# Odd mixer of a two-layer network: the norm's factor in the stream, the gate read from its bank, softplus as a scale

## Chip, cores and metric

The kernel runs on one core of a Trainium2 chip. What counts is the device time of one execution in microseconds (us). Matmuls run on TensorE (PE in the rows), the other work on VectorE (DVE), ScalarE (ACT) and GpSimd (POOL); SyncE (SP) issues most DMAs.

## The reference

The network takes 512 tokens of 1024 channels in fp32 through an even mixer, an odd mixer and other blocks around them. The change is in the odd mixer. Cut to what matters:

```python
def odd_mixer(h, w_in, conv_w, conv_b, w_rg, b_rg, w_ig, b_ig, lam, w_out):
    p = einsum("btd,dn->btn", h, w_in)            # h is rmsnorm(h, g): h * rsqrt(mean(h*h) + eps) * g
    xr, gate = split(p, [1536], axis=-1)
    xc = causal_depthwise_conv(xr, conv_w, conv_b)          # 4 taps
    r = sigmoid(per_head(xc, w_rg) + b_rg)                  # 12 heads of 128
    i = sigmoid(per_head(xc, w_ig) + b_ig)
    log_a = -8.0 * r * softplus(-lam)
    a = exp(log_a)
    mult = sqrt(-expm1(2.0 * log_a))
    bterm = mult * (i * xc)
    hs = scan(a, bterm)                                     # h_t = a_t * h_(t-1) + b_t
    y = hs * silu(gate)
    return einsum("btn,nd->btd", y, w_out)
```

## The kernel before

**Layout.** Activations stand transposed: a tile is 128 channels by 512 tokens, so the stream of 1024 channels is 8 tiles, and each of the 12 heads is one tile. Every fp32 matmul is made of three: an operand is split in a rounded high part and the rest, and `mm3` (lines 303 to 310) multiplies high by high (308), high by low (309) and low by high (310). A head's input projection is `mtile`: 8 tiles by 3, so 24 matmuls into one bank.

**Weights.** A chunk of weights is loaded by SyncE's queue into one of two raw buffers (line 288), cast on ScalarE to its high part (`hi<-raw`, recorded at the helper's line 249), and its low part is a subtraction, in this stage on GpSimd (`lo<-raw,hi`, helper line 252). hi and lo have three buffers each; the small gate weights of a head (`wrh`, `wrl`) one. The kernel asks for a chunk three ahead of its use.

**The odd stage** is `odd`, from line 733. The stream times g is split in 8 tiles xg, each with a high and a low part. The squares of h are summed, PE turns the sum into columns (line 368), VectorE makes the reciprocal root `rs_s` of them, PE spreads it (line 397), and ScalarE copies it to the tile `rs`, the norm's factor for each token. The loop runs over 12 heads with a lag of 3: head n+3's projection goes into one of three "mm" banks, is multiplied by `rs` in the bank, convolved (one ScalarE activation and three VectorE steps that read the bank, `xc<-mm,vecs,xc`) and split to `xs`; then for head n the two gate products r and i (6 matmuls, two "sp" banks), two sigmoids, the product of r by `sp4` (4 times softplus) and of i by xc on GpSimd, and the gate projection into one of two "yp" banks (24 matmuls), which VectorE multiplies by `rs` into `gt`.

After each second head `lru` (line 787) does the recurrence of two heads on tiles of 1024, the 12 heads making six groups, 0 to 5. On ScalarE: tanh of the gate, tanh and exp of x, sqrt. On VectorE: two steps `u<-u,e`, two products for x, two scans (line 808), the product with the gate, and the split to y. x, i and gt have two buffers; e and u have one. ScalarE needs another table for sigmoid, exp and sqrt (ACT_TABLE_LOAD), while tanh goes with more than one of them.

The out-projection follows: 8 output tiles of two weight chunks each, first the chunks of heads 0 to 5 for seven of the tiles (the first half), then those of heads 6 to 11 (the second half). It reuses the banks of all three names.

**Order of the work.** Instructions are put on the engines' queues by a scheduler with a timeline of its own (line 1822), not in the order of the code; `lru` is put behind by `later`. Each engine then works strictly in its order. A small change in the code can so move many instructions, and the section on the change shows what stands where.

## Time and profile before

| | |
|---|---|
| runs shown | 1882.61, 1886.52, 1893.18 us; median 1886.52 |
| profiled execution | 1886.16 us; its span 1884.3 us |
| granted TensorE clock, mean of the span | 0.963 |
| TensorE busy | 1764.2 us (94%) |
| VectorE busy | 1167.2 us (62%) |
| ScalarE busy | 762.0 us (40%) |
| GpSimd busy | 456.6 us (24%) |
| the odd stage | 425.7 to 697.9 us of the span |

The profile is of one execution. Start times are counted from the first instruction; the span leaves out the 1.86 us around it. A row of a timeline gives the start, the duration, the engine, the kernel's line, the operation, the tiles (written <- read), and in brackets how long the engine was idle before it and what it waited for. A row with x3 stands for three instructions that follow each other. Rows of waits and groups give sums. Successive instructions of an engine overlap a little, so the distance between two starts is shorter than the duration.

### The profile page before, as it was taken

The page shows a single profiled execution, that of the slowest core. Times are in us where ns is not written, and L with a number is a line of the kernel's source. Part 1 is how long each engine was busy: PE and PEld are TensorE (multiplying, and loading weights), DVE is VectorE, ACT ScalarE, POOL GpSimd, SP SyncE. Part 2 cuts the span into 40 slices and gives each one's busy share as a digit, 9 for nine tenths or more (in the row PEclk, how much of TensorE's full clock was granted, in tenths as well). Part 3 has the DMA queues.
Part 4 walks back from the last instruction along what each step waited for, and adds up shares of the span by engine and source line. Part 5 has one row for each costly group of instructions (what it writes and reads, how often), then busy time and mean ns, then how long its engine had stood idle before and what let it go on. Part 6 is the DMA issues. An engine that isn't in the chain of part 4 may idle for free.

```text
span 1884.3 us, 24650 instructions
## 1 busy us (share of the span) xinstructions
PE 1764.2 (94%) x9298; PEld 1439.7 (76%) x9298; DVE 1167.2 (62%) x1885; ACT 762.0 (40%) x1330; POOL 456.6 (24%) x422
## 2 busy tenths in 40 slices
PE   7797999999887897899999999998999999999997
PEld 5685778877765776687888888887778888888886
DVE  9989777555888859655432344578686642244456
ACT  4334444443554462234432332335665432233234
POOL 5464667333666643100000000032000000000002
PEclk8898999999988898899999999999999999999998
DMA  4598443331222488523232222333111233322322
GB/s 167 136 225 213 128 129 123 119 104 65 76 75 76 136 244 291 169 92 112 93 100 91 100 100 91 101 106 110 41 55 45 101 101 91 100 101 91 100 94 91
DMA packets 128871, 215.93 MB, mean 115 GB/s; under 512 B 40048, under 2 KB 79728, under 8 KB 128752
## 3 DMA queue, kind: packets, MB, share of 16 engines
q1 hardware_dynamic: 108144, 189.27, 32.5%
q10 hardware_dynamic: 17968, 16.43, 2.6%
q0 software_dynamic: 2640, 8.65, 1.4%
q8 instruction: 73, 1.20, 0.3%
q14 instruction: 46, 0.38, 0.1%
HBM read 187.44 MB, written 26.21 MB: 113 GB/s over the span
## 4 chain that ended last, share of the span: by engine, by line
PE 68%; DVE 14%; issue 5%; POOL 4%; ACT 4%; DMA 3%; SPq 1%; ACTq 0%; DVEq 0%; POOLq 0%
PE mm L308 19%; PE mm L310 19%; PE mm L309 19%; POOL lo L252 2%; DVE lo L252 1%; DVE e L808 1%; ACT hi L249 1%; PE pv L1609 1%; SPq L1175 1%; PE sc L309 1%; PE sc L308 1%; PE sc L310 1%; DVE pl L264 1%; DVE srm L267 1%; DVE h L264 1%
## 5 line engine op out<-in xcount | busy, mean ns | idle before, releaser
L249 ACT ACTIVATE hi<-raw 128x1024 fp32r<-128x1024 f32 (+1 forms) x280 | 292.4, 1046 | 672.8 <-PE mm L309 552.4
L252 DVE TENSOR_TENSOR lo<-raw,hi 128x1024 fp32r<-128x1024 f32 (+1 forms) x211 | 262.1, 1243 | 422.1 <-ACT hi L249 417.3
L310 PE MATMUL mm<-xg,lo 128*128 128x512 f32 x924 | 361.0, 391 | 9.4 <-DVE lo L252 8.1
L308 PE MATMUL mm<-xg,hi 128*128 128x512 f32 x924 | 363.2, 394 | 5.1 <-ACT hi L249 1.8
L309 PE MATMUL mm<-xg,hi 128*128 128x512 f32 x924 | 360.2, 390 | 0.3 <-DVE xg L252 0.2
L1423 POOL DMA_DIRECT2D pj<-proj x16 | 8.8, 549 | 1025.8 <-DVE t L264 784.0
L308 PE MATMUL mm<-hid,hi 128*128 128x512 f32 (+1 forms) x648 | 250.7, 387 | 1.8 <-DVE t L252 1.8
L309 PE MATMUL mm<-hid,hi 128*128 128x512 f32 (+1 forms) x648 | 250.3, 387 | 0.0
L310 PE MATMUL mm<-hid,lo 128*128 128x512 f32 (+1 forms) x648 | 250.1, 386 | 0.0
L310 PEld LDWEIGHTS mm<-xg,lo 128*128 128x128 f32 x924 | 173.8, 188 | 48.0 <-DVE lo L252 9.0
L308 PEld LDWEIGHTS mm<-xg,hi 128*128 128x128 f32 x924 | 173.8, 188 | 44.9 <-ACT hi L249 2.3
L252 POOL TENSOR_TENSOR lo<-raw,hi 128x1024 fp32r<-128x1024 f32 (+1 forms) x69 | 170.6, 2473 | 146.8 <-ACT hi L249 140.6
L309 PEld LDWEIGHTS mm<-xg,hi 128*128 128x128 f32 x924 | 173.8, 188 | 36.4 <-DVE xg L252 1.4
L308 PEld LDWEIGHTS mm<-hid,hi 128*128 128x128 f32 x648 | 121.7, 188 | 26.6 <-DVE t L252 2.0
L310 PEld LDWEIGHTS mm<-hid,lo 128*128 128x128 f32 x648 | 121.7, 188 | 24.6
L309 PEld LDWEIGHTS mm<-hid,hi 128*128 128x128 f32 x648 | 121.7, 188 | 24.6
L308 PE MATMUL mm<-y,hi 128*128 128x512 f32 x192 | 78.6, 409 | 10.2 <-ACT y L249 8.9
L309 PE MATMUL mm<-y,hi 128*128 128x512 f32 x192 | 76.8, 400 | 0.0
L310 PE MATMUL mm<-y,lo 128*128 128x512 f32 x192 | 76.5, 399 | 0.0
L309 PE MATMUL mm<-big,hi 128*128 128x512 f32 x160 | 64.5, 403 | 3.9 <-DVE big L264 3.9
L308 PE MATMUL mm<-big,hi 128*128 128x512 f32 x160 | 65.3, 411 | 2.2 <-ACT hi L249 2.2
L310 PE MATMUL mm<-big,lo 128*128 128x512 f32 x160 | 64.2, 402 | 0.1
(468 smaller groups left out, 3086.1 us busy)
## 6 DMA issues: line engine op xcount, KB each, us to landing
raw<-in_w_up SPq DMA_DIRECT2D x64, 512.0 KB
raw<-in_w_down SPq DMA_DIRECT2D x64, 512.0 KB
raw<-in_w_in_even SPq DMA_DIRECT2D x40, 512.0 KB
raw<-in_w_in_odd SPq DMA_DIRECT2D x24, 512.0 KB
raw<-in_w_out_even SPq DMA_DIRECT2D x16, 512.0 KB
raw<-in_w_glu SPq DMA_DIRECT2D x16, 512.0 KB
raw<-in_w_gate SPq DMA_DIRECT2D x16, 512.0 KB
raw<-in_w_out_odd SPq DMA_DIRECT2D x16, 384.0 KB
```

Source lines behind the costliest of these rows:

```text
L249: self.nc.scalar.activation(out=out, in_=in_, func=func, scale=scale, bias=bias)
L252: (eng or self.nc.vector).tensor_tensor(out=out, in0=a, in1=b, op=op)
L264: self.nc.vector.scalar_tensor_tensor(out=out, in0=a, scalar=s, in1=b, op0=op0, op1=op1)
L267: (eng or self.nc.vector).tensor_scalar(out=out, in0=a, scalar1=s1, scalar2=s2, op0=op0, **({} if op1 is None else {"op1": op1}))
L308: mm(out, hi[:, sl], xh, start=start, stop=False)
L309: mm(out, hi[:, sl], xl, start=False, stop=False)
L310: mm(out, lo[:, sl], xh, start=False, stop=stop)
L808: nc.vector.tensor_tensor_scan(out=y, data0=u[:, k], data1=x[:, k], initial=0.0, op0=ALU.mult, op1=ALU.add)
L1175: nc.sync.dma_start(out=M0[:, 128 * g:128 * g + 128], in_=bass.AP(k0.tensor, k0.offset + 4096 * g, [[16, 8], [256, 16], [1, 128]]))
L1423: self.nc.gpsimd.dma_start(out=p, in_=pj[m])
L1609: mm(o, l, r[:, w], start=n == 0, stop=n == 6 * nk - 1)
```

## The change

Three things in `odd` and `lru`:

- The first four heads (0 to 3) still read the raw stream, which now lies in the buffers of y, and are multiplied by `rs` in the bank. After head 0's convolution the code makes a second stream, `xn`, split from h times g times `rs` (8 products, 8 casts, 8 subtractions); heads 4 to 11 and all gate projections read it and are not multiplied any more. The new lines at the top of `odd` only allocate tiles, which fixes their addresses.
- The gate's tanh reads the bank directly, per head, and one VectorE step makes (tanh + 1) times the bank. The product by `rs` and the tanh and product of 1024 in `lru` are gone.
- GpSimd's product of x by `sp4` is gone. tanh and exp in `lru` run per head, on 512 tokens, with a column of `sp4` as the activation's scale; `sp4` has 24 columns, 12 for tanh and 12 for exp.

```diff
     def odd(self, h):
         nc = self.nc
-        xg = [self.split(h[k], self.X(), self.V("g_odd", k)) for k in range(8)]
+        for t, b, w in (("acc", 2, T), ("xr", self.XR, T), ("rs", 1, T), ("xc", 2 + self.LAG, T), ("xs", 2 + 2 * self.LAG, T), ("wrh", 1, 256),
+                        ("wrl", 1, 256), *((t, b, self.G * T) for t, b in (("x", 2), ("i", 2), ("gt", 2), ("e", 1), ("u", 1)))):
+            self.L(t, b, F32, (128, w))
+        xg = [self.split(h[k], self.LR("y", 24), self.V("g_odd", k)) for k in range(8)]
...
-                self.mul(px, px, rs)
+                if n <= self.LAG:
+                    self.mul(px, px, rs)
...
+                if n == 0:
+                    xn = []
+                    for k in range(8):
+                        if k % 2 == 0:
+                            t2 = self.L("gt", 2, F32, (128, G, T))
+                        t = t2[:, k % 2]
+                        self.stt(t, h[k], self.V("g_odd", k), rs, ALU.mult, ALU.mult)
+                        xn.append(self.split(t, self.X()))
+                if n == self.LAG:
+                    xg = xn
                 n -= self.LAG
...
-            self.ts(x, x, self.sp4[:, n:n + 1], ALU.mult, 0.0, ALU.add, eng=nc.gpsimd)
             self.mul(i, i, xc, nc.gpsimd)
             pg = self.mtile(xg, "yp")
-            self.mul(gt, pg, rs)
+            self.act(gt, pg, AF.Tanh, scale=0.5)
+            self.stt(gt, gt, 1.0, pg, ALU.add, ALU.mult)
             if n % G == G - 1:
                 with self.later(self.LRU):
-                    ysp += self.lru(*grp)
+                    ysp += self.lru(n - G + 1, *grp)
...
-    def lru(self, x, i, gt):
+    def lru(self, n, x, i, gt):
...
-        self.act(u, gt, AF.Tanh, scale=0.5)
-        self.stt(gt, u, 1.0, gt, ALU.add, ALU.mult)
-        self.act(u, x, AF.Tanh)
-        self.act(e, x, AF.Exp, scale=-2.0)
+        for k in range(self.G):
+            self.act(u[:, k], x[:, k], AF.Tanh, scale=self.sp4[:, n + k:n + k + 1])
+        for k in range(self.G):
+            self.act(e[:, k], x[:, k], AF.Exp, scale=self.sp4[:, 12 + n + k:13 + n + k])
         self.act(x, u, AF.Sqrt)
...
-        self.sp4 = C("sp4", 12)
-        self.ts(self.sp4, q, 4.0, ALU.mult)
+        self.sp4 = C("sp4", 24)
+        self.ts(self.sp4[:, 0:12], q, 4.0, ALU.mult)
+        self.ts(self.sp4[:, 12:24], q, -8.0, ALU.mult)
```

How the scheduler places this is seen at three places. In the names of the rows, `sp_628` is `sp4` and `vecs` holds constants.

**The start of the stage.** VectorE before, from the end of the reciprocal root: three bank products, then convolutions of heads 0 to 2 and one gate.

```order
L264 SCALAR_TENSOR_TENSOR rs_s<-rs_s 128x4
L252 TENSOR_TENSOR mm<-mm,rs 128x512 x3
L264 SCALAR_TENSOR_TENSOR xc<-mm,vecs,xc 128x509
L252 TENSOR_TENSOR gt<-yp,rs 128x512
L264 SCALAR_TENSOR_TENSOR xc<-mm,vecs,xc 128x509
L264 SCALAR_TENSOR_TENSOR xc<-mm,vecs,xc 128x510
```

VectorE of the change, from the same place to the last convolution step of head 0, the first of 128x511:

```order
L264 SCALAR_TENSOR_TENSOR rs_s<-rs_s 128x4
L252 TENSOR_TENSOR mm<-mm,rs 128x512
L264 SCALAR_TENSOR_TENSOR gt<-h,vecs,rs 128x512 x4
L252 TENSOR_TENSOR mm<-mm,rs 128x512 x2
L264 SCALAR_TENSOR_TENSOR xc<-mm,vecs,xc 128x509
L252 TENSOR_TENSOR xg<-gt,xg 128x512 x3
L264 SCALAR_TENSOR_TENSOR xc<-mm,vecs,xc 128x509
L264 SCALAR_TENSOR_TENSOR xc<-mm,vecs,xc 128x510
L252 TENSOR_TENSOR xg<-gt,xg 128x512
L264 SCALAR_TENSOR_TENSOR xc<-mm,vecs,xc 128x509
L264 SCALAR_TENSOR_TENSOR gt<-h,vecs,rs 128x512 x2
L264 SCALAR_TENSOR_TENSOR xc<-mm,vecs,xc 128x510
L264 SCALAR_TENSOR_TENSOR xc<-mm,vecs,xc 128x511
```

The products and subtractions of the second stream (`gt<-h,vecs,rs`, `xg<-gt,xg`) now stand between the convolutions. PE of the change at the end of its first gate matmuls (`xg` is the second stream here, `y` the raw one):

```order
L309 MATMUL yp<-xg,hi 128x512
L310 MATMUL yp<-xg,lo 128x512
L308 MATMUL yp<-xg,hi 128x512
L308 MATMUL mm<-y,hi 128x512
L309 MATMUL mm<-y,hi 128x512
```

Here head 3's projection (`mm<-y`) begins after 13 gate matmuls; before, it began after 45 of them, the whole gate of head 0 and most of head 1's. The columns (line 368) came after 52 head matmuls before and come after 62 now; the spread (line 397) came after a further 20 head and 11 gate matmuls before, and comes after 10 head matmuls now.

**One cycle on ScalarE.** Before, from group 1's exp to its sqrt and the next sigmoid:

```order
L249 ACT_TABLE_LOAD
L249 ACTIVATE e<-x 128x1024
L249 ACTIVATE hi<-raw 128x1024
L249 ACTIVATE u<-gt 128x1024
L249 ACTIVATE u<-x 128x1024
L249 ACT_TABLE_LOAD
L249 ACTIVATE x<-u 128x1024
L249 ACT_TABLE_LOAD
L249 ACTIVATE x<-sp,vecs 128x512
```

The same stretch of the change:

```order
L249 ACT_TABLE_LOAD
L249 ACTIVATE e<-x,sp_628 128x512
L249 ACT_TABLE_LOAD
L249 ACTIVATE x<-sp,vecs 128x512
L249 ACTIVATE wrh<-raw 128x256
L249 ACTIVATE i<-sp,vecs 128x512
L249 ACTIVATE hi<-raw 128x1024
L249 ACTIVATE u<-x,sp_628 128x512
L249 ACT_TABLE_LOAD
L249 ACTIVATE e<-x,sp_628 128x512
L249 ACT_TABLE_LOAD
L249 ACTIVATE x<-u 128x1024
```

The two heads' exp stand apart, with the second head's sigmoids and one cast between them. In the whole stage there were 19 table loads and there are 33.

**The end of the loop on ScalarE.** Before, around group 5's sqrt (`x<-u`):

```order
L249 ACTIVATE hi<-raw 128x768
L249 ACTIVATE u<-gt 128x1024
L249 ACTIVATE hi<-raw 128x768
L249 ACTIVATE u<-x 128x1024
L249 ACT_TABLE_LOAD
L249 ACTIVATE e<-x 128x1024
L249 ACT_TABLE_LOAD
L249 ACTIVATE x<-u 128x1024
L249 ACTIVATE hi<-raw 128x768 x7
```

The same place of the change:

```order
L249 ACTIVATE u<-x,sp_628 128x512
L249 ACT_TABLE_LOAD
L249 ACTIVATE e<-x,sp_628 128x512 x2
L249 ACT_TABLE_LOAD
L249 ACTIVATE x<-u 128x1024
L249 ACTIVATE hi<-raw 128x768
L249 ACT_TABLE_LOAD
L249 ACTIVATE gt<-yp 128x512
L249 ACTIVATE hi<-raw 128x768 x8
```

Of the out-projection's chunks (`hi<-raw 128x768`) four were cast before group 5's sqrt; now two are.

## Rows read from the trace of the kernel before

**Rows 1.** The page's first part: busy time, share of the span, instructions.

```profile
PE 1764.2 (94%) x9298; PEld 1439.7 (76%) x9298; DVE 1167.2 (62%) x1885; ACT 762.0 (40%) x1330; POOL 456.6 (24%) x422
```

**Rows 2.** Waits of PE, 437 to 720 us: total us, times, longest.

```profile
PE sp L308 <- ACT wrh L249: 10.5, 3, 6.1
PE yp L310 <- POOL lo L252: 7.5, 6, 2.7
```

**Rows 3.** Windows, cut at each group's first `u<-u,e`; last: PEclk, DMA share, GB/s.

```profile
437.50:459.70 22.20, 18.79 (x82) 15.00 (x81) 14.84 (x30) 5.36 (x7) 7.69 (x4) 0.92 0.23 77
459.70:486.80 27.10, 27.10 (x120) 22.15 (x118) 12.00 (x15) 15.51 (x19) 14.54 (x10) 1.00 0.14 49
486.80:522.20 35.40, 30.34 (x129) 23.80 (x129) 31.13 (x28) 16.61 (x20) 21.48 (x13) 1.00 0.24 82
522.20:556.00 33.80, 28.73 (x109) 22.20 (x109) 28.00 (x27) 16.46 (x20) 21.78 (x12) 0.85 0.20 70
556.00:587.30 31.30, 24.75 (x88) 17.58 (x86) 26.92 (x27) 16.54 (x20) 20.88 (x12) 0.89 0.18 61
587.30:617.00 29.70, 20.80 (x71) 15.94 (x72) 22.34 (x21) 16.45 (x21) 20.42 (x13) 0.79 0.34 105
617.00:641.00 24.00, 21.80 (x92) 17.24 (x90) 19.94 (x15) 12.46 (x14) 16.01 (x8) 0.97 0.44 132
...
658.20:698.10 39.90, 39.86 (x175) 32.39 (x173) 24.48 (x29) 22.69 (x35) 18.96 (x18) 1.00 0.80 243
```

**Rows 4.** Timeline of ACT in the first cycle.

```profile
511.69 1.28 ACT L249 ACT_TABLE_LOAD   x1 [3.07 <-DVE y L252]
...
518.65 1.06 ACT L249 ACTIVATE u<-x 128x1024 f32<-128x1024 f32 x1 [2.71 <-DVE gt L264]
519.73 1.28 ACT L249 ACT_TABLE_LOAD   x1
521.02 1.06 ACT L249 ACTIVATE x<-u 128x1024 f32<-128x1024 f32 x1
```

**Rows 5.** Groups of DVE, 425 to 680 us: busy, mean ns, idle time before them.

```profile
L264 DVE SCALAR_TENSOR_TENSOR u<-u,e 128x1024 f32<-128x1024 f32 x12 | 18.0, 1499 | 20.0 <-ACT x L249 19.8
...
L252 DVE TENSOR_TENSOR x<-x,i 128x1024 f32<-128x1024 f32 x6 | 12.0, 1997 | 0.1
...
L264 DVE SCALAR_TENSOR_TENSOR gt<-u,gt 128x1024 f32<-128x1024 f32 x6 | 11.5, 1910 | 7.6 <-ACT u L249 7.6
L264 DVE SCALAR_TENSOR_TENSOR e<-e,gt 128x512 f32<-128x512 f32 x12 | 10.4, 902 | 0.0
...
L264 DVE SCALAR_TENSOR_TENSOR xc<-mm,vecs,xc 128x509 f32<-128x509 f32 x12 | 8.9, 742 | 5.8 <-ACT xc L249 5.6
...
L252 DVE TENSOR_TENSOR gt<-yp,rs 128x512 f32<-128x512 f32 x12 | 8.2, 680 | 0.7 <-PE yp L310 0.7
L252 DVE TENSOR_TENSOR mm<-mm,rs 128x512 f32<-128x512 f32 x12 | 8.1, 689 | 11.6 <-PE mm L310 6.7 <-ACT rs L249 4.9
```

**Rows 6.** Timeline of PE: head 3's first matmul, and the second half's.

```profile
459.71 0.40 PE L308 MATMUL mm<-xg,hi 128*128 128x512 f32 x1
...
658.22 0.39 PE L308 MATMUL mm<-y,hi 128*128 128x512 f32 x1
```

**Rows 7.** Timeline of DVE at the start of the stage.

```profile
447.20 1.90 DVE L252 TENSOR_TENSOR mm<-mm,rs 128x512 f32<-128x512 f32 x3 [4.92 <-ACT rs L249]
...
450.26 4.67 DVE L264 SCALAR_TENSOR_TENSOR xc<-mm,vecs,xc 128x509 f32<-128x509 f32 x7
```

**Rows 8.** Groups of ACT, 425 to 680 us, as in rows 5.

```profile
L249 ACT ACT_TABLE_LOAD x19 | 24.4, 1283 | 12.8 <-DVE y L252 12.5
```

**Rows 9.** Timeline of DVE in group 5, behind the last head.

```profile
647.72 1.22 DVE L252 TENSOR_TENSOR x<-x,i 128x1024 f32<-128x1024 f32 x1
649.88 3.97 DVE L808 TENSOR_TENSOR_SCAN e<-u,x 128x512 f32<-128x512 f32 x2 [0.94 <-POOL u L267]
```

**Rows 10.** Groups of POOL, 425 to 680 us, as in rows 5.

```profile
L267 POOL TENSOR_SCALAR x<-x,sp 128x512 f32<-128x512 f32 x12 | 13.9, 1159 | 19.1 <-ACT x L249 19.1
```

## The prediction

> **What bounds the kernel now.** I read the page's first part, then TensorE's waits in the odd stage, then the windows cut at each group's first recurrence step, and last the timelines of ScalarE and VectorE inside one cycle. TensorE is busy for 94% of the span [rows 1], and the matmuls stay the same in number; the change can pay only where TensorE waits. In the odd stage it does, for casts and subtractions of weights (10.5 us and 7.5 us are the largest two) [rows 2]. These come late because ScalarE and GpSimd do them between the steps of the recurrence. The windows show it: each of the five cycles from one group's first recurrence step to the next lasts 35.4, 33.8, 31.3, 29.7 and 24.0 us (154.2 in all, mean 30.8), TensorE is busy for only 20.8 to 30.3 of these and has lost granted clock (1.00 down to 0.79) [rows 3]. No engine is full there. What turns is a loop: e and u have one buffer each, so a group's exp on ScalarE waits for the last y of the group before (the table load at 511.69, idle until y) [rows 4], then tanh, load, sqrt (the sqrt at 521.02) [rows 4], and VectorE's recurrence steps wait for that sqrt, 19.8 us over six groups [rows 5]. I split each cycle at the last y: the VectorE chain, first step to last y, takes 24.7, 20.7, 19.8, 19.0, 20.3 (mean 20.9), and the ScalarE chain, y to next first step, takes 10.7, 13.1, 11.5, 10.7, 3.6 (mean 9.9). The loop ends when group 5 has had its sqrt; the weights of the out-projection are cast behind it on ScalarE, and its second half starts at 658.22 [rows 6]. From there TensorE is full at clock 1.00 to 698.1 [rows 3].
>
> **The start of the stage.** The change puts the norm's factor into the stream right after head 0, so VectorE gets 8 scaled products and 8 subtractions more, between the convolutions of heads 0 to 2; TensorE's order now has 13 gate matmuls, then all of head 3, where it had 45 gate matmuls first. Head 3 needs a bank that head 0's convolution must free. In the new order 19 VectorE instructions stand before that point. At 0.63 us (three took 1.90) to 0.67 us (seven took 4.67) [rows 7] that is 12.2 us. They start about 446.1: the columns' sums come after 62 head matmuls and not 52, 2.3 us later at 0.226 each (120 in 27.1 us [rows 3]), but the spread no longer stands behind twenty head and eleven gate matmuls, so the factor arrives a little before the 447.2 at which VectorE's wait of 4.92 us for it ended [rows 7]. Head 3 then starts at 458.3, against 459.71 [rows 6], with 32 gate matmuls (7.2 us) still to do, and TensorE idle for some 11 us ahead of it. That the clock falls with such a gap I take at 2 us (22.2 us at 0.92 around the gaps there now, 1.8 lost [rows 3]). To the second head's r and i product 94 matmuls then stand in the new order (21.2 us): 481.5. Behind it on ScalarE are two sigmoids, two tanh, load, exp, load and sqrt: by starts, 0.58 for a half tile, 1.28 a load, 1.06 the sqrt [rows 4, 8]: 6.7 and a hand-over, 7.3 in all. Group 0's first step thus comes at 488.8, 2 us later than 486.8. Ends: 0 if the later gate matmuls fill gaps in any case, 7 if all 32 are missed.
>
> **The cycle on VectorE.** Removed per group: one gate product of 1024 (1.91), two products by the factor (0.68 each) and, from head 4 on, two bank products (0.69 each) [rows 5]; added: two gate products of 512 that read a bank. No row shows one; the nearest are the convolution step, which reads a bank too (0.74), and e times gt (0.90) [rows 5]. I take 0.74, since its operands are of the same kind. Per group that is 4.65 off and 1.5 on. Most of what leaves stood in ScalarE's half of the cycle or beside it, so I did not book it but laid out the new order with the shortest time of each kind. Between first step and last y of the first cycle this gives: two steps 2.3, three convolution steps 1.95, x 1.6, x times i 1.2, two scans 4.0 (3.97 in the tail [rows 9]), cast and subtraction of the head 1.0, gate product 0.66, two e 1.3, y 2.2, and 1.3 of waiting for GpSimd's u: 17.5. The same for the others gives 19.7, 17.1, 16.6 and 15.6.
>
> These are undisturbed times. The same x times i takes 1.22 at best and 2.00 in the mean [rows 5, 9], and the recurrence rows together took some 4 us more per group than their shortest. GpSimd's share of that falls, because the product by softplus goes (12 of 1.16 us, 2.3 per group, of some 20 us that it is busy in a cycle [rows 3, 10]). Between 0 and 4 I add 2.2 per group: 19.7, 21.9, 19.3, 18.8, 17.8, mean 19.5.
>
> **The cycle on ScalarE.** Removed: one tanh of 1024 for the gate and, with it, the wait for VectorE's gate product (2.71 us at 518.65) [rows 4]. Added: tanh and exp in halves, the gate's tanh per head, and table loads, 33 in the stage where there were 19, because sigmoid, tanh and exp now alternate head by head; each load is 1.28 [rows 8]. In the new order the first cycle's exp of one head waits for y; behind it come load, sigmoid, small cast, sigmoid, cast, tanh, load, exp, load, sqrt. In the spacings above that is 0.58 + 1.28 + 0.58 + 0.31 + 0.57 + 0.95 + 0.58 + 1.28 + 0.69 + 1.28 + 1.06, about 9, against 10.6 before. Written out alike, the five are 8.9, 9.7, 11.4, 8.6 and 3.3 (mean 8.4): the third load takes back most of what the gate's wait gave.
>
> **The sum.** Cycles of 28.6, 31.6, 30.7, 27.4 and 21.1 make 139.4 (154.2 before), so group 5's first step comes at 488.8 + 139.4 = 628.2, where it came at 641.0. Of these 12.8 us not all arrive. The new order casts only two weight chunks of the out-projection ahead of group 5's sqrt, where the old one cast four. So five chunks remain behind it: one cast and the first low part, 3.4, and 90 matmuls at 0.2255, 20.3. The second half starts at 628.2 + 23.7 = 651.9, 6.3 us before 658.22. From there the rows stay, so 1886.16 (the profiled execution, 0.36 below the median 1886.52) becomes 1879.9, say **1880**. The turning point: group 5's first step before 634.5, a mean cycle below 29.1.
>
> Costed at nothing: the factor's ScalarE casts (8 of about 0.7), which lie where TensorE waits for VectorE; the second softplus column (one 12-wide VectorE row in an earlier stage); the raw stream in the y tiles, which no unfinished reader holds; and what heads 4 to 11 gain by a convolution that starts without the bank product, since the loop and not the bank holds them. If the 8 casts came into the open, they would cost 5.6.
>
> **Bounds.** With no interference the cycles sum to 128.4, the step comes at 617.2, the second half at 640.9: 1868.8. With no start loss, 1866.8. With cycles as before (154.2) it comes at 666.7: 1894.6.
>
> **Rivals.** *A, slower: the loop gets longer on ScalarE.* VectorE's chain stays at 20.9, because the scans and products are held up by GpSimd's weight subtractions as before, and ScalarE's grows from 9.9 to 11.2 by the third load. Five cycles of 32.1 are 160.5, the step comes at 649.3, the second half at 673.0: 1886.2 + 14.8 = 1901. It decides from a mean cycle of 29.1 up. For it: three loads stand between y and sqrt where two did, and the changed order puts sigmoids and a cast between them. Against it: the gate's wait of 2.71 is gone [rows 4]. With half of this it ends near 1895.
>
> *A', the loads cost more than they show.* If the engine emptied after a load for as long again (1.28), the 13 loads in the ScalarE chains add 16.6: about 1896.5. The rows speak against it: load at 519.73, next activation at 521.02 [rows 4]. The Trainium skill (ScalarE: Activation LUTs, What ACT_TABLE_LOAD costs) puts a switch at a load of 1283 ns and a drain of 1380 ns behind it; with 13 drains the time would be 1898, an estimate from that page. The load agrees with [rows 8], a drain behind it is not seen.
>
> *B, faster: less GpSimd work lets VectorE run undisturbed.* Cycles of 128.4 in all, 1869. For it: products in the tail, beside an idle GpSimd, take 1.22 [rows 9]. Against it: GpSimd keeps nine tenths of its work. The Trainium skill (SBUF — State Buffer, SBUF: two separate sides) has a VectorE instruction with two SBUF inputs and GpSimd share a port pair as an exclusive lock, so that one blocks the other for a whole instruction. By that rule the 2.3 us of the removed product would come off each of five cycles, an estimate of 11.5 in all, between the forecast and B; the spread of 1.22 to 2.00 [rows 5, 9] is of that kind.
>
> *C, no change: the loop turns faster, but the weights set the end.* In the last 40 us the DMA engines are at 0.80 [rows 3]. If the chunks arrive no earlier, the second half starts at 658 whatever the loop does: 1886. Against it: TensorE was full there, so arrival had not yet bound it.
>
> **How the numbers follow.** Forecast 0.50 (1874 to 1886), B 0.20, C 0.14, A 0.13, A' 0.03. About 0.5%, 9.4 us, is what a measurement tells from no change. Faster than that (below 1877): B and a quarter of the forecast, 0.32. Slower (above 1895.6): most of A, and A', 0.13. The rest 0.55. The range takes in B with its early start and the lower part of A: 1865 to 1898.
>
> **What would show it.** Head 3 starting near 458 after a wait for VectorE; group first steps at about 489, 517, 549, 580, 607 and 628; 33 table loads of 1.28 in the stage; GpSimd without the softplus product and x times i nearer to 1.2 than to 2.0; the second half at 652. I am wrong if group 5's step is not before 634 (A), if it is early and the second half still starts at 658 (C), or if head 3 starts after 465, since then the start costs more than the loop gives.

## The result and the profile after

The changed kernel takes 1897.13 us (median of 12), the kernel before 1885.99 in the same comparison: a ratio of 1.0069, with an interval of 1.0058 to 1.0080. It is slower by 0.7%, where 1880 was forecast. The ratios compare the fast executions alone and so are not the quotients of the medians; one of the twelve before, of 7523.35 us, is not among them. The profiled execution took 1897.36 us, its span 1895.5.

The page's first part of the changed kernel, beside [rows 1]:

```profile
PE 1761.9 (93%) x9298; PEld 1438.1 (76%) x9298; DVE 1155.9 (61%) x1888; ACT 788.9 (42%) x1370; POOL 438.7 (23%) x410
```

VectorE and GpSimd have less to do (11 and 18 us) and ScalarE more (27 us). The loss is not in the sums, then, but in when things happen. The windows of the changed kernel, cut at the same events as [rows 3] (the columns after the clock and those of busy time are as there):

```profile
437.50:467.40 29.90, 18.16 (x72) 13.84 (x70) 20.04 (x34) 9.08 (x13) 7.15 (x3) 0.77 0.12 40
467.40:500.10 32.70, 32.70 (x137) 26.90 (x138) 19.08 (x28) 20.20 (x26) 12.32 (x8) 0.95 0.17 57
500.10:530.90 30.80, 26.57 (x104) 20.02 (x104) 23.93 (x23) 19.29 (x24) 19.71 (x10) 0.92 0.24 77
530.90:563.00 32.10, 25.69 (x105) 19.56 (x103) 24.60 (x24) 21.11 (x26) 18.83 (x10) 0.97 0.20 70
563.00:594.40 31.40, 26.95 (x102) 21.32 (x103) 25.07 (x24) 20.99 (x26) 18.66 (x11) 0.89 0.19 63
594.40:623.10 28.70, 20.93 (x76) 15.81 (x76) 20.14 (x20) 18.60 (x23) 13.66 (x9) 0.88 0.30 102
623.10:647.50 24.40, 18.88 (x81) 14.48 (x79) 18.30 (x14) 15.25 (x20) 14.90 (x8) 1.00 0.42 130
647.50:673.90 26.40, 23.62 (x90) 18.53 (x91) 15.86 (x13) 6.67 (x8) 14.68 (x7) 0.87 0.50 149
673.90:714.90 41.00, 40.98 (x181) 33.61 (x179) 25.66 (x30) 24.07 (x38) 19.50 (x19) 1.00 0.75 232
```

Head 3 starts at 467.4 (459.7 before) and group 0's first step comes at 500.2 (486.8 before), 13.3 us late. The five cycles then last 30.8, 32.1, 31.4, 28.7 and 24.4, 147.4 in all against 154.2: the loop does turn faster, and 6.8 of the 13.3 are won back. Group 5's first step is at 647.5, 6.6 us late. From there to the second half it takes 26.4 us, 17.3 before, so that starts at 673.9, 15.7 late.

What happens at the start stands in VectorE's timeline of the changed kernel, beside [rows 7], and in GpSimd's (one row):

```profile
445.54 0.16 DVE L267 TENSOR_SCALAR v_s<-st 128x4 f32<-128x4 f32 x1 [6.65 <-PE st L368]
...
446.92 2.53 DVE L264 SCALAR_TENSOR_TENSOR rs_s<-rs_s 128x4 f32<-128x4 f32 x2
449.49 2.26 DVE L252 TENSOR_TENSOR rs_s<-rs_s,v_s 128x4 f32<-128x4 f32 x1
451.78 0.16 DVE L264 SCALAR_TENSOR_TENSOR rs_s<-rs_s 128x4 f32<-128x4 f32 x1
454.81 0.70 DVE L252 TENSOR_TENSOR mm<-mm,rs 128x512 f32<-128x512 f32 x1 [2.86 <-ACT rs L249]
```

```profile
447.07 4.66 POOL L252 TENSOR_TENSOR lo<-raw,hi 128x1024 fp32r<-128x1024 f32 x2 [13.79 <-ACT hi L249]
```

The columns' sums reach VectorE at 445.5 (438.5 before), and the small rows of the reciprocal root, 0.16 us elsewhere in the same list, take 2.5 for two and 2.3 for one beside GpSimd's weight subtractions. So the factor is multiplied in at 454.8 and not at 447.2. TensorE shows where the first part of that comes from; its timeline in the changed kernel, rows with a wait, one of the slow matmuls behind the first two waits, and head 3's first:

```profile
427.02 0.97 PE L308 MATMUL mm<-y,hi 128*128 128x512 f32 x3 [1.58 <-ACT y L249]
429.42 0.50 PE L309 MATMUL mm<-y,hi 128*128 128x512 f32 x1 [1.43 <-DVE y L264]
...
430.66 0.63 PE L309 MATMUL mm<-y,hi 128*128 128x512 f32 x1
...
452.09 2.05 PE L397 MATMUL st<-ctile,rs_s 128*128 128x128 f32 x8 [4.15 <-DVE rs_s L264]
456.89 0.80 PE L308 MATMUL yp<-xg,hi 128*128 128x512 f32 x1 [2.75 <-ACT xg L249]
460.96 0.80 PE L309 MATMUL yp<-xg,hi 128*128 128x512 f32 x1 [3.28 <-DVE xg L252]
...
467.37 0.51 PE L308 MATMUL mm<-y,hi 128*128 128x512 f32 x1 [0.81 <-DVE xc L264]
```

It starts the stage by waiting for the raw stream. ScalarE split the first tile of it at 396.40 before, while the even mixer still ran, and splits it at 426.27 now:

```profile
396.40 0.70 ACT L249 ACTIVATE xg<-h,vecs 128x512 fp32r<-128x512 f32 x1
```

```profile
426.27 0.71 ACT L249 ACTIVATE y<-h,vecs 128x512 fp32r<-128x512 f32 x1
```

(The first is the kernel before, the second the changed one.) The old buffers belong to the whole program; the y tiles belong to the odd stage, in a place that the even mixer's stage uses for tiles of its own, and in the new order the scheduler put all eight splits behind that stage. After that TensorE waits for the factor, for the second stream and for head 0's convolution in turn.

### The profile page after: what moved, and what is told of

Its sections match the earlier page's. It is cut to its first block, busy times and chain, and to the rows that moved or that the text cites. A ratio compares the mean times of both kernels' runs of the same rounds, so it can differ in the third digit from the quotient of the medians.

```text
span 1895.5 us, 24696 instructions
## 1 busy us (share of the span) xinstructions
PE 1761.9 (93%) x9298; PEld 1438.1 (76%) x9298; DVE 1155.9 (61%) x1888; ACT 788.9 (42%) x1370; POOL 438.7 (23%) x410
## 4 chain that ended last, share of the span: by engine, by line
PE 66%; DVE 14%; ACT 6%; issue 4%; POOL 4%; DMA 3%; SPq 1%; ACTq 0%; DVEq 0%; POOLq 0%
PE mm L308 19%; PE mm L310 19%; PE mm L309 19%; DVE e L824 1%; POOL lo L252 1%; DVE lo L252 1%; PE pv L1626 1%; ACT hi L249 1%; ACT L249 1%; DVE xs L252 1%; SPq L1192 1%; PE sc L309 1%; PE sc L308 1%; PE sc L310 1%; DVE h L264 1%
## 5 line engine op out<-in xcount | busy, mean ns | idle before, releaser
L310 PE MATMUL mm<-xg,lo 128*128 128x512 f32 x892 | 350.2, 393 | 9.6 <-DVE lo L252 7.7
L308 PE MATMUL mm<-xg,hi 128*128 128x512 f32 x892 | 351.1, 395 | 4.6 <-ACT hi L249 3.1
L309 PE MATMUL mm<-xg,hi 128*128 128x512 f32 x892 | 348.7, 391 | 0.0
L310 PEld LDWEIGHTS mm<-xg,lo 128*128 128x128 f32 x892 | 168.5, 189 | 46.6 <-DVE lo L252 8.5
L308 PEld LDWEIGHTS mm<-xg,hi 128*128 128x128 f32 x892 | 168.6, 189 | 42.6 <-ACT hi L249 3.9
L309 PEld LDWEIGHTS mm<-xg,hi 128*128 128x128 f32 x892 | 168.4, 189 | 35.1 <-DVE xg L252 0.6
L308 PE MATMUL mm<-y,hi 128*128 128x512 f32 x224 | 91.6, 415 | 15.2 <-ACT y L249 10.6
L309 PE MATMUL mm<-y,hi 128*128 128x512 f32 x224 | 90.8, 405 | 1.4 <-DVE y L264 1.4
L310 PE MATMUL mm<-y,lo 128*128 128x512 f32 x224 | 90.7, 405 | 1.4 <-POOL lo L252 1.4
L308 PEld LDWEIGHTS mm<-y,hi 128*128 128x128 f32 x224 | 44.2, 198 | 27.3 <-ACT y L249 11.8
```

The lines of the kernel that those rows point to most:

```text
L308: mm(out, hi[:, sl], xh, start=start, stop=False)
L309: mm(out, hi[:, sl], xl, start=False, stop=False)
L310: mm(out, lo[:, sl], xh, start=False, stop=stop)
```

## The experiments

All compare with the kernel before, run on the same chip (medians of 1884.2 to 1885.6 us); a run's ratio is given with its interval. Places in the span are from one profiled execution of each kernel. Two theories stood at first: S, the start is lost by the factor in the stream; L, the added table loads lose the time.

**Without the factor.** The change's second and third part alone (shown against the changed kernel; the lines that allocate tiles first and make `xn` are gone too):

```diff
-        xg = [self.split(h[k], self.LR("y", 24), self.V("g_odd", k)) for k in range(8)]
+        xg = [self.split(h[k], self.X(), self.V("g_odd", k)) for k in range(8)]
...
-                if n <= self.LAG:
-                    self.mul(px, px, rs)
+                self.mul(px, px, rs)
...
             pg = self.mtile(xg, "yp")
+            self.mul(pg, pg, rs)
             self.act(gt, pg, AF.Tanh, scale=0.5)
```

> The change without its first part: one raw stream in its old buffers, every head and every gate multiplied by the norm's factor in the bank; the gate's tanh from the bank and softplus as a scale stay. Theory S (the start): what made the change slower is the factor in the stream, which put group 0's first step at 500.2 instead of 486.8. Then this run has that step at 486 to 489, cycles summing to about 147 as in the changed kernel, group 5's step at 634 and a time 5 to 8 us below before. Theory L (the loads): the table loads and half-width activations lose the time, wherever the factor stands. Then this run, with 28 loads against 19, stays 8 us or more above before.

1880.47 us, 0.9978 (0.9968 to 0.9988). First step at 482.9, cycles 149.0, group 5's step at 631.9, the second half at 655.8 (23.9 behind it). Theory S holds, with a first step 3 us earlier than it asked: the factor in the stream, with all that came with it, costs 16.7 us of 1897, and what remains of the change is a gain. Theory L falls as the cause, for 28 of the 33 loads were here.

**Scale alone.** The kernel before with the third part only:

```diff
-            self.ts(x, x, self.sp4[:, n:n + 1], ALU.mult, 0.0, ALU.add, eng=nc.gpsimd)
...
-        self.act(u, x, AF.Tanh)
-        self.act(e, x, AF.Exp, scale=-2.0)
+        for k in range(self.G):
+            self.act(u[:, k], x[:, k], AF.Tanh, scale=self.sp4[:, n + k:n + k + 1])
+        for k in range(self.G):
+            self.act(e[:, k], x[:, k], AF.Exp, scale=self.sp4[:, 12 + n + k:13 + n + k])
```

> Only the third part on the kernel before: GpSimd's product by softplus gone, tanh and exp per head with a scale, 23 loads. Theory S: the first step near 487, the cycles a little shorter since GpSimd has 2.3 us less per group, time 0 to 5 us below before. Theory L: each of the 4 more loads and the halves are paid on the path, 5 us or more above before.

1887.60 us, 1.0014 (1.0004 to 1.0023): a little slower, between what the two theories asked. Cycles of 33.0, 35.2, 32.5, 35.5 and 22.9, 159.0 in all. GpSimd's 2.3 us per group bought nothing; VectorE waited for the sqrt for longer than before (25.2 us in five waits against 19.8 in six [rows 5]).

**Gate alone.** The second part only:

```diff
             pg = self.mtile(xg, "yp")
-            self.mul(gt, pg, rs)
+            self.mul(pg, pg, rs)
+            self.act(gt, pg, AF.Tanh, scale=0.5)
+            self.stt(gt, gt, 1.0, pg, ALU.add, ALU.mult)
...
-        self.act(u, gt, AF.Tanh, scale=0.5)
-        self.stt(gt, u, 1.0, gt, ALU.add, ALU.mult)
```

> Only the second part on the kernel before: every gate multiplied by the factor in its bank, tanh read from the bank, one product per head; softplus stays on GpSimd, 22 loads. Theory G (the gain of the run without the factor is the gate's, since the scale alone lost 2 us): 4 to 7 us below before, 1879 to 1882. Rival: the two parts need each other, since with both GpSimd and ScalarE's wait for the gate are relieved; then within 1.5 us of before.

1877.71 us, 0.9963 (0.9949 to 0.9977), cycles 145.2. The gain is the gate's.

**Scale with the two exps together.** Added to the run without the factor:

```diff
-        for k in range(self.G):
-            self.act(e[:, k], x[:, k], AF.Exp, scale=self.sp4[:, 12 + n + k:13 + n + k])
+        with self.after(mybir.EngineType.Activation):
+          for k in range(self.G):
+            self.act(e[:, k], x[:, k], AF.Exp, scale=self.sp4[:, 12 + n + k:13 + n + k])
```

> The run without the factor, with a group's two exps issued only behind its second tanh, so that they stand together: 22 loads in place of 28. Theory L2 (the scale part cost its 2 to 3 us by loads in ScalarE's path): 1877 to 1878, as the run with the gate alone (1877.7). Rival: the exp that comes early was hidden and the late one is not, or the product by softplus was no loss on GpSimd; then 1880 or more.

1878.29 us, 0.9958 (0.9945 to 0.9971), cycles 146.2 against 149.0. The interval just touches that of the run without the factor (0.9968 to 0.9988), so it is likely and not shown that the scale's loss was its early exp and the loads around it. Beside the gate alone (0.9963), the scale with the exps together costs nothing that can be told, and gains nothing.

**First gates on the raw stream.** The changed kernel, gates 0 and 1 on the raw stream and multiplied in the bank.

```diff
-            pg = self.mtile(xg, "yp")
+            pg = self.mtile(raw if n < 2 else xg, "yp")
+            if n < 2:
+                self.mul(pg, pg, rs)
```

> The changed kernel, with the gates of heads 0 and 1 on the raw stream and multiplied in the bank, so that TensorE has 47 gate matmuls ahead of head 3 (13 in the change). The raw stream still lies in the y tiles and starts late. Theory S: TensorE's idle of some 11 us before head 3 is filled, group 0's first step comes 4 to 8 us before the changed kernel's 500.2, and the time is 4 to 8 us below the changed kernel's 1897. Theory L: 32 loads as before, so 1897 within 3.

1895.81 us, 1.0056 (1.0044 to 1.0069), first step at 498.75. A miss for theory S; the time is the one that L asked, but L had fallen with the first run. TensorE's gap ahead of head 3 was filled in part only: within the 47 gate matmuls it stood 5.9 us for a cast of weights, and head 3 came at 475.6. Counted from the even mixer's end the first step is 3.6 us earlier than in the change, but the ratio (1.0069 there) differs by less than the intervals.

**Raw stream in its old buffers.** In addition to the last edit, so that the second stream follows in the same ring behind head 3:

```diff
-        raw = xg = [self.split(h[k], self.LR("y", 24), self.V("g_odd", k)) for k in range(8)]
+        raw = xg = [self.split(h[k], self.X(), self.V("g_odd", k)) for k in range(8)]
```

> The changed kernel with the raw stream in its old buffers, so that it can be split while the even mixer still runs, gates 0 and 1 on it too, and the second stream in the same buffers as the raw tiles come free behind head 3. Theory S1 (the start is lost by the raw stream's late split): group 0's first step at 483 to 488 and a time of 1879 to 1885. Theory S2 (it is lost by the 16 VectorE rows and 8 casts of the second stream, wherever the raw one lies): first step at 490 or later and 1886 to 1892.

1882.40 us, 0.9988 (0.9978 to 0.9999), first step at 484.5: S1's numbers. But both the early split and the second stream's place differ from the change.

**Raw stream late, first try.** On the kernel before:

```diff
-        xg = [self.split(h[k], self.X(), self.V("g_odd", k)) for k in range(8)]
+        with self.after():
+            xg = [self.split(h[k], self.X(), self.V("g_odd", k)) for k in range(8)]
```

> The kernel before, with one edit: the raw stream's splits may be issued only behind the last matmul of the even mixer, as they are in the changed kernel. Theory S1: the columns' sums come 3 to 5 us later, group 0's first step at 490 to 492, the time 3 to 5 us above before. Theory S2: within 1 us of before.

1884.72 us, 1.0000 (0.9989 to 1.0012). It tells nothing: the edit did not move the splits (ScalarE's first still ran in the even mixer), so this was the kernel before once more.

**Raw stream late, alone.** All splits now read a copy of g that depends on the last tile of h:

```diff
+        g2 = self.p_s.tile([128, 8], F32, tag="g2", name="g2", bufs=1)
+        self.stt(g2, h[7][:, 0:8], 0.0, self.V("g_odd", 0, 8), ALU.mult, ALU.add)
-        xg = [self.split(h[k], self.X(), self.V("g_odd", k)) for k in range(8)]
+        xg = [self.split(h[k], self.X(), g2[:, k:k + 1]) for k in range(8)]
```

> The kernel before, with the weights g of the norm passed through one small step that also reads the last tile of h, so that every split of the raw stream waits for the end of the even mixer, as in the changed kernel. Same buffers, same work but for that step. Theory S1 (the late raw stream): v_s at 442 to 445 instead of 438.5, group 0's first step at 491 to 495, the time 4 to 8 us above before. Theory S2 (the second stream's work): v_s at most 1 us later, the time within 1.5 us of before.

1888.28 us, 1.0007 (0.9997 to 1.0016). v_s at 444.3 as S1 said, yet the first step at 486.0, no later than before, and a time that the interval does not tell from before: S1's first half holds, its second does not. The scheduler saw the late split and reordered: head 3 stood behind 24 gate matmuls and not 45, the small rows of the root met no GpSimd work, and the factor was multiplied in at 450.08:

```profile
444.31 0.16 DVE L267 TENSOR_SCALAR v_s<-st 128x4 f32<-128x4 f32 x1 [5.36 <-PE st L368]
...
450.08 1.90 DVE L252 TENSOR_TENSOR mm<-mm,rs 128x512 f32<-128x512 f32 x3 [3.63 <-ACT rs L249]
```

**Second stream's work alone.** On the kernel before, in the loop over heads:

```diff
+                if n == 0:
+                    for k in range(8):
+                        if k % 2 == 0:
+                            t2 = self.L("gt", 2, F32, (128, G, T))
+                        t = t2[:, k % 2]
+                        self.stt(t, h[k], self.V("g_odd", k), rs, ALU.mult, ALU.mult)
+                        self.split(t, self.LR("y", 24))
```

> The kernel before, with the second stream's 8 products, 8 casts and 8 subtractions made behind head 0 as in the change, written to y tiles and read by nobody; all heads and gates stay on the raw stream, which is split early. It adds work and computes the same output. Theory S2: group 0's first step 5 to 7 us later (491 to 494), the time 5 us or more above before. Theory S1: the 16 rows lie beside the 45 gate matmuls that stand ahead of head 3, first step within 3 us of 487, the time 0 to 4 us above before.

1888.42 us, 1.0015 (1.0004 to 1.0025). The first step stands at 494.0, as S2 asked, but in the profiled execution the even mixer itself ended 3.5 us later; counted from there, the step is 3.6 us late, between the theories, and the time is within S1's 0 to 4 us. By the second half's start this is gone (the table below), and behind it 1231.0 us follow, 1226.1 before; what holds them was not followed up.

**Raw early, second stream first.** The changed kernel with buffers exchanged:

```diff
-        xg = [self.split(h[k], self.LR("y", 24), self.V("g_odd", k)) for k in range(8)]
+        xg = [self.split(h[k], self.X(), self.V("g_odd", k)) for k in range(8)]
...
-                        xn.append(self.split(t, self.X()))
+                        xn.append(self.split(t, self.LR("y", 24)))
...
-            ys.append(self.halves(y, self.LR("y", 24)))
+            ys.append(self.halves(y, self.LR("y", 24) if n < 4 else self.X()))
...
-            U = self.p_xg.tile([128, 8, 64], F32, tag="xg", name="U")
+            U = self.L("y", 24, F32, (128, 8, 64))
```

> The changed kernel with the buffers exchanged: the raw stream in its old buffers, split early, the second stream in 16 of the y tiles, the later y in the raw stream's buffers. TensorE's order at the start is the change's (13 gate matmuls on the second stream, then head 3) but the columns come after 52 head matmuls, as before. Theory S1 (the factor arrives 7.6 us late, because the raw stream does, and all of that is carried on): v_s near 438.5, group 0's first step at 491 to 494. Theory S2 (gates and head 3 wait for the second stream's work): first step at 497 or later. Whole time 1889 to 1891 by S1, 1895 or more by S2.

1889.01 us, 1.0020 (1.0010 to 1.0029). The time is the one S1 asked, but not on its grounds. First step at 485.6, earlier than S1 had it:

```profile
437.27 0.16 DVE L267 TENSOR_SCALAR v_s<-st 128x4 f32<-128x4 f32 x1 [2.93 <-PE st L368]
...
443.50 0.70 DVE L252 TENSOR_TENSOR mm<-mm,rs 128x512 f32<-128x512 f32 x1 [2.36 <-ACT rs L249]
...
485.60 4.57 DVE L264 SCALAR_TENSOR_TENSOR u<-u,e 128x1024 f32<-128x1024 f32 x2 [3.85 <-ACT x L249]
```

TensorE's order (13 gate matmuls, then head 3) and the second stream's work ahead of it are the change's, and the first step is not late. So the exchange of buffers is worth the whole delay at the start, and 1.0069 became 1.0020. What is left over before does not stand at the start: the cycles are 148.9, and from group 5's first step to the second half it takes 26.0 us, 17.3 before.

**Raw late, second stream later.** On the run with the first gates raw:

```diff
-                if n == 0:
+                if n == self.LAG:
                     xn = []
```

> The changed kernel with gates 0 and 1 on the raw stream and the second stream made behind head 3 and not behind head 0; the raw stream still in the y tiles and late. Theory S1: first step as in the run with the first gates raw (498.75), or 1 to 2 us before, 1893 to 1896. Theory S2: first step 6 us or more before that, at 493 or earlier, 1887 to 1890.

1895.96 us, 1.0052 (1.0038 to 1.0067). First step at 500.5, as S1 had it: the place of the second stream makes no difference that can be told while the raw stream is late.

```profile
448.64 0.16 DVE L267 TENSOR_SCALAR v_s<-st 128x4 f32<-128x4 f32 x1 [6.63 <-PE st L368]
...
457.00 0.70 DVE L252 TENSOR_TENSOR mm<-mm,rs 128x512 f32<-128x512 f32 x1 [1.94 <-ACT rs L249]
```

The start of all these runs, and the start of the out-projection's second half, in us from the end of the even mixer's last matmul (from 424.7 to 429.4 in the span, so that starts of different executions compare):

| kernel | v_s | factor multiplied in | group 0's first step | second half | ratio to before |
|---|---|---|---|---|---|
| before | 12.6 | 21.3 | 61.0 | 232.3 | 1 |
| change | 20.1 | 29.4 | 74.7 | 248.5 | 1.0069 |
| without the factor | 12.6 | 21.3 | 56.5 | 229.4 | 0.9978 |
| first gates raw | 20.0 | 28.4 | 71.1 | 244.7 | 1.0056 |
| raw in old buffers | 12.6 | 21.3 | 59.6 | 232.7 | 0.9988 |
| raw late alone | 18.9 | 24.7 | 60.6 | 228.8 | 1.0007 |
| second stream's work alone | 12.6 | 21.3 | 64.6 | 230.1 | 1.0015 |
| raw early, second stream first | 12.6 | 18.8 | 60.9 | 235.8 | 1.0020 |
| raw late, second stream later | 20.1 | 28.4 | 71.9 | 245.4 | 1.0052 |

The three kernels whose factor comes at 28 or later are the three that lose half a per cent or more. They are also the three with the raw stream in the y tiles, so the table alone does not tell the late factor from whatever else goes with these tiles.

A second thing sets the end. Of the 126 matmuls of the out-projection's first half 54 were left at group 5's first step before, and 90 are left in the change. In every kernel here whose gate reads its bank 72 to 99 are left, and 23.1 to 26.4 us pass from that step to the second half; in the others 50 to 54, and 13.0 to 17.6 us. So a part of what the loop wins in these kernels is TensorE's work put behind it: the gate alone shortens the cycles by 9.0 us and pays 6.9 there.

**Scan into x.** The kernel before, `y = e[:, k]` becoming `y = x[:, k]`.

> The kernel before, with the scan writing into x (two buffers) and not into e (one buffer); nothing else, and the same 19 loads. Theory E (the loop runs through e's single buffer): the next group's exp no longer waits for the last y, the wait of ScalarE for y goes, the ScalarE chain falls from 9.9 to 5 or 6 per cycle, and the time falls by 10 to 25 us, until TensorE's 24.4 us per two heads bound the cycle. Rival: u, also single, holds the loop as well (tanh waits for the scans), or VectorE is what fills the cycle; then under 4 us.

1890.11 us, 1.0030 (1.0018 to 1.0042), cycles 154.4: theory E falls for the kernel before. ScalarE's timeline of this run tells why:

```profile
540.40 0.78 ACT L249 ACTIVATE xc<-mm,vecs 128x512 f32<-128x512 f32 x1 [10.32 <-DVE mm L252]
...
543.03 1.28 ACT L249 ACT_TABLE_LOAD   x1
544.32 1.06 ACT L249 ACTIVATE e<-x 128x1024 f32<-128x1024 f32 x1
```

The exp, free of y now, stands in ScalarE's order behind a convolution's start, and that waits 10.3 us for VectorE's bank product, which stands behind the recurrence. So e's buffer was one of two things that held it there. The 4 us over before are not in the loop: they lie behind the second half's start (1230.0 us to the end, 1226.1 before) and were not followed up.

**u and e freed early.** The run without the factor, and:

```diff
-        self.ts(u, u, -2.0, ALU.mult, -1.0, ALU.add, eng=nc.gpsimd)
+        self.ts(e, u, -2.0, ALU.mult, -1.0, ALU.add, eng=nc.gpsimd)
...
-            y = e[:, k]
-            nc.vector.tensor_tensor_scan(out=y, data0=u[:, k], data1=x[:, k], initial=0.0, op0=ALU.mult, op1=ALU.add)
+            y = x[:, k]
+            nc.vector.tensor_tensor_scan(out=y, data0=e[:, k], data1=x[:, k], initial=0.0, op0=ALU.mult, op1=ALU.add)
```

> The run without the factor, with the last GpSimd step of the recurrence writing into e and the scan reading e and writing into x (two buffers): u is free before the scans, e behind them. In that run tanh waited for the scan for 21.0 us in five cycles. Theory E2 (u's one buffer holds the loop there): cycles shorter by 3 to 4 us each, the time 6 to 14 us below that run's 1880.5. Rival: exp, which now waits for the scans, or VectorE's own work takes the place of that wait: 1880 within 3.

1875.05 us, 0.9947 (0.9931 to 0.9963), cycles 141.0 against 149.0, 1.6 each where E2 asked 3 to 4. It lies a little short of E2's 6 to 14 us (5.4), and it has 35 table loads, 28 without the edit. ScalarE's waits between 480 and 650 us (total, times, longest), first without, then with the edit:

```profile
ACT u L249 <- DVE e L809: 21.0, 5, 5.6
```

```profile
ACT gt L249 <- DVE yp L252: 17.4, 4, 7.0
...
ACT e L249 <- DVE x L809: 8.5, 4, 3.3
...
ACT u L249 <- POOL e L267: 3.6, 2, 2.1
```

Tanh's wait for the scan is gone (21.0; 3.6 for GpSimd's step are left), and exp has one instead (8.5): the buffer held the loop, and part of the gain went to the next wait.

**The same edit on the gate alone.**

> The gate part alone, with u and e freed early as in the run that did this with gate and scale. Theory E2 (the single buffers hold the loop in every variant): 3 to 6 us below the gate-only run's 1877.7, so 1872 to 1875, the fastest of all. Rival: there tanh is one row of 1024 that waits for GpSimd's product anyway, and nothing is gained: within 1.5 us of 1877.7.

1876.86 us, 0.9948 (0.9935 to 0.9961), cycles 140.6 against 145.2. From 0.9963 the step lies within the intervals, as the rival had it, and E2's 3 to 6 us are not seen in the time; in the profile the loop is shorter by 4.5 us.

**The same edit on the run with the exps together.**

> No factor in the stream, gate from its bank, softplus as a scale, the two exps together (22 loads), and u and e freed early. If the two gains add (2.2 us by the exps, 5.4 us by the buffers, from 1880.5): 1873. If the loads are hidden once the buffers are free: 1875 as in the run with the buffers alone.

1875.96 us, 0.9951 (0.9939 to 0.9964), cycles 138.9. The gains do not add. The three runs with freed buffers (0.9947, 0.9948, 0.9951) can't be told apart; each beats the kernel before by half a per cent and the change by 1.2%.

## Why the prediction was wrong

By its own sum, step by step, against the profiled execution of the changed kernel:

| term | predicted | measured |
|---|---|---|
| columns' sums at VectorE | 440.8 | 445.5 |
| factor multiplied in | 446.1 | 454.8 |
| 19 VectorE instructions to head 0's bank | 12.2 | 12.6 |
| head 3 starts | 458.3 | 467.4 |
| group 0's first step | 488.8 | 500.2 |
| five cycles | 139.4 | 147.4 |
| group 5's first step | 628.2 | 647.5 |
| from there to the second half | 23.7 | 26.4 |
| second half starts | 651.9 | 673.9 |
| from there to the end | 1227.9 | 1223.5 |

**The step that failed first** is "The start of the stage", and in it a cost put at nothing: "the raw stream in the y tiles, which no unfinished reader holds". I asked whether a reader held the tiles and not when the scheduler would place the splits. The first of them moved by 30 us, behind the even mixer. The prediction had seen that the columns follow 62 head matmuls (2.3 us) but let these start as before and run without a stop. In the change they wait 3.0 us at first, and the 59 behind these waits take 15.1 us, 0.26 each: eight of them stood 0.43 us apart at a granted clock of 0.50, the lower of its two levels (430.2 to 433.3), the rest 0.23. That makes the 4.7 us of the first line. The small rows beside GpSimd's subtractions add 2.6 over before. From them to the multiplied bank it took 2.9 us where I had 1.5; the eight matmuls of the spread took 2.05 there at a granted clock of 0.50, and 1.05 before at 1.00. So the factor came 8.7 us after the forecast, and everything behind it kept that. Of the other 2.7 us to group 0's first step 2.5 stand on ScalarE: from the second head's last product (490.4) it took 9.8 us to the step, where I had 7.3, and ahead of the sigmoids stood a cast that waited for its weights and one table load more:

```profile
490.92 1.06 ACT L249 ACTIVATE hi<-raw 128x1024 fp32r<-128x1024 f32 x1 [2.07 <-DMA raw<-in_w_in_odd]
492.00 1.28 ACT L249 ACT_TABLE_LOAD   x1
493.30 0.69 ACT L249 ACTIVATE x<-sp,vecs 128x512 f32<-128x512 f32 x1
```

Taking the late split away by an exchange of buffers won the whole delay of the first step back, with the second stream still ahead of head 3, and 0.5% of the time. Moving the second stream alone won nothing, and more gate matmuls ahead of head 3 won 3.6 us at the first step and little time. So the loss needs the late split. The late split by itself, with all gates on the raw stream, became only 3.4 us on the factor, and the scheduler's other order made up for them, so it does not lose the time alone: it does so with the order of the change. Of the 13.7 us by which the first step is late, counted from the even mixer, 8.1 are the factor's and 5.6 arise behind it. How they divide between the late split, the ten more matmuls, the small rows and the order was not separated, and why the order of the run with the late split alone absorbs it was not followed further.

**The second step that failed** is the loop, below, and it would have lost the side without the first. Taking the start's 11.4 us off the 1897.4 gives 1886, no change. And the run with the raw stream early and the second stream first has its first step at 485.6, ahead of the forecast's 488.8, and yet took 1889.0 (its later y tiles lie in other buffers too).

**The second stream** was costed nearly rightly: 12.2 us forecast for the run of VectorE rows, 12.6 measured, and the run with its work alone is late by 3.6 us at the first step where I had booked 2 for the start.

**The loop** had the right sign and half the size: 6.8 us of 14.8. VectorE's part came to 20.5 on average (19.5 forecast, 20.9 before). Groups of VectorE in the changed kernel, 425 to 690 us, beside [rows 5]:

```profile
L824 DVE TENSOR_TENSOR_SCAN e<-u,x 128x512 f32<-128x512 f32 x12 | 30.7, 2595 | 5.6 <-POOL u L267 5.6
L264 DVE SCALAR_TENSOR_TENSOR u<-u,e 128x1024 f32<-128x1024 f32 x12 | 20.9, 1741 | 29.5 <-ACT x L249 29.4
...
L252 DVE TENSOR_TENSOR x<-x,i 128x1024 f32<-128x1024 f32 x6 | 8.2, 1365 | 0.2
L264 DVE SCALAR_TENSOR_TENSOR gt<-gt,yp 128x512 f32<-128x512 f32 x12 | 8.2, 681 | 6.6 <-ACT gt L249 6.3
```

x times i is down from 2.00 to 1.37, as said, and the gate's product costs 0.68 (0.74 taken). But the scans stayed slow (2.6 us), and the first steps became slower (1.74): GpSimd's time was not removed from VectorE's way, it met other rows. Two first steps took 4.56 us at 500.17, where a subtraction of weights began at 501.1, and 2.48 at 594.43, where the last one had just ended. The "shortest time of each kind" was misread for the scans. The pair of [rows 9], 3.97 us, was not undisturbed: it began with a subtraction of GpSimd beside it, and its first scan took 2.86, its second 1.19. VectorE and then GpSimd in the kernel before:

```profile
652.66 1.19 DVE L808 TENSOR_TENSOR_SCAN e<-u,x 128x512 f32<-128x512 f32 x1
```

```profile
649.82 1.84 POOL L252 TENSOR_TENSOR lo<-raw,hi 128x768 fp32r<-128x768 f32 x1
```

So 1.6 us of meetings with GpSimd were in the base already, the bound "with no interference" was not one, and the 2.2 us per group put on for GpSimd were too few: the mis-sized term is VectorE's by 1.0 us a cycle and ScalarE's by 0.6. ScalarE's part came to 9.0 (8.4 forecast). Its waits in the changed kernel, 480 to 650 us:

```profile
ACT u L249 <- DVE e L824: 21.1, 5, 5.0
ACT e L249 <- DVE y L252: 14.9, 5, 4.5
```

The larger wait is for u's buffer, which the prediction named but did not charge: it had only exp waiting, for e.

**The tail** was 2.7 us short: TensorE waited twice behind the sqrt, and the matmuls from 650.5 to 656.0 ran at a granted clock of 0.55 (0.87 over the whole 26.4 us), where I had all 90 at full speed. TensorE's timeline of the changed kernel, beside [rows 6]:

```profile
648.23 0.50 PE L308 MATMUL mm<-y,hi 128*128 128x512 f32 x1 [3.86 <-ACT hi L249]
650.49 0.80 PE L310 MATMUL mm<-y,lo 128*128 128x512 f32 x1 [1.36 <-POOL lo L252]
...
673.91 0.39 PE L308 MATMUL mm<-y,hi 128*128 128x512 f32 x1
```

4.5 us came back behind the second half.

**The rivals.** A' had the nearest number (1896.5) by luck, and A (1901, or 1895 with half of it) the next; both had the wrong place. A is refuted by the cycles: the loop did not lengthen. A' is refuted by its own row; 33 loads took 1.283 each, and behind 28 of them the next activation follows 1.29 to 1.30 us after the load's start (the other five are exps that waited for VectorE's y), so no drain of the kind that the Trainium skill gives (ScalarE: Activation LUTs, What ACT_TABLE_LOAD costs) is seen here:

```profile
L249 ACT ACT_TABLE_LOAD x33 | 42.3, 1283 | 0.5
```

B's mechanism showed in one group of rows and was lost in another. C did not come into play: of TensorE's 5.9 us of waits between group 5's first step and the second half 5.2 stand right behind the sqrt, in the two rows above. No rival had the late raw stream in it. That the measured time lies within 1865 to 1898 is owed to the lower part of A, which set the upper end, and not to a mechanism that came true.

## What to carry to other kernels

A tile that is moved to other buffers may be written at another time: ask which stage owns the new buffers and read the new order for the first write of that tile, not only for the work around it. Where everything behind a point needs one small result (here the norm's factor), price each thing that delays that result at full length, and each piece of work that could run without it as cover. Of a change in three parts, one can lose more than the other two gain; running the parts apart gave 0.4% with three lines moved (the gate), and half a per cent with the buffers freed. And a loop that turns faster wins only what it does not leave to be done behind it: count the work of the busiest engine that is still open when the loop ends.

## What was not expected of the hardware

Rows of 128 by 4 elements on VectorE, 0.16 us by themselves, took 2.26 us once and 2.53 for two beside two GpSimd subtractions that took 4.66 together, and the slow rows ended with the subtractions (449.45 and 451.75; the second subtraction ended at 451.73). In the kernel before one such row took 1.83 us (at 438.69) beside a pair of subtractions that ended with it, so the price was there to be read. The Trainium skill (SBUF — State Buffer, SBUF: two separate sides) has a VectorE instruction with two SBUF inputs and a GpSimd instruction that reads SBUF block one another, for the whole of the one that started first; a GpSimd row of 2.3 us is about what one small row took. That the price falls on rows so small, in the one chain that all else waits for, the forecast had left out.
